# A hybrid layer on one core: x, four weights and B in one chain of loads, gates moved forward, Toeplitz matrices copied inside SBUF, C loaded once, and TensorE's order fixed in the output stage

## The chip, the core and the metric

The kernel runs on one core of a Trainium2 chip. The metric is the device time of one execution in microseconds (us); less is better. TensorE (PE) does the matmuls, VectorE (DVE), ScalarE (ACT) and GpSimd (POOL) the rest, and DMAs are issued from queues that belong to SyncE (SP), ACT or POOL.

## What is computed

One layer on x of 512 positions by 1024 columns, in float32. h = RMSNorm(x) goes through one projection w_in whose columns are split among a state-space branch with a gate, an attention branch with three head groups and a gate, and two merge gates:

```
h = rms_norm(x, norm_w)
u_s, z_s, q, k, v, z_a, r_s, r_a = split(h @ w_in)
y_s = s5_branch(u_s, lam, log_dt, b, c, d_skip, w_glu)      # GLU(GELU(Re(C h) + D u))
y_s = (y_s * silu(z_s)) @ w_ssm_out
y_a = dilated_attention(rope(norm(q)), rope(norm(k)), v)
y_a = (y_a * silu(z_a)) @ w_attn_out
m = sigmoid(r_s) * y_s + sigmoid(r_a) * y_a
out = x + m @ w_o
```

The state-space branch has 64 groups of 16 channels and 64 complex states each. Its recurrence runs over the 512 positions with a diagonal matrix that does not depend on the data.

## The kernel before, in words

Every product that matters is three fp32r matmuls: both sides are split into a high part and a low part, and mm3 (lines 107 to 110) adds high by high, high by low and low by high. cm_unit (line 180) makes 128 output columns for all 512 positions in 24 matmuls. `plan` fixes the order of the weights; load_w (line 170) loads one from SP into two rotating buffers `w_raw`, ACT makes `w_hi` (line 93), DVE makes `w_lo` (line 95). A Tile scheduler orders each engine's instructions from the program and its own estimates; POOL, ACT and SP each serve their list in order, and so do their DMA queues.

The stages follow one another:
- **Start** (196 to 240): x in four pieces, sums of squares, scaling (224), transposes to hT and their split. SP's list mixes the loads of x, the first two weights, the lambdas, B in four loads (419 to 422), positions and norm weights.
- **u units** 0 to 7 (264), and beside them the lambda chain on DVE, whose powers reach TensorE as atp and ftp and come back as AT and fT; from these and B come BB and BB2 on POOL and DVE.
- **W and X units** (271, 283): coefficients `ab` (coef, 252), their transposes (wps, 279), a copy W, and the input of the scan.
- **Scan** on DVE (589 to 648). TensorE runs gates ("fillers") meanwhile: `order` has za, zs, V of head pair 0, rs and two ra.
- **M stage** (675 to 793). For j = 0 to 7: ca_unit makes the output coefficients from C; m_unit makes kps on TensorE, copies it to `kt` on ACT (710), adds the diagonal on POOL (711), stores it to DRAM (kd, 712) and reads it back as the Toeplitz matrix (dd<-kd, 715); s_unit copies the scan's states (728, 729); y_unit makes yps from both (739, 741); g_unit transposes ysb and does the GELU in ACT and DVE. The gates' outputs go to DRAM (gd, rad) from SP (472, 478, 486).
- **GLU and w_ssm_out**, then **attention** over four head pairs: q and k of three groups, their turning (qtp, 847), scores with softmax (903 to 967), values (970: transposes ptp, then ot). Group weights are made on DVE (948 to 956) and moved across partitions by 16 POOL copies (960). V of pairs 1 to 3 is computed together with the third group of q and k.
- **The end**: w_attn_out with the gate loads `ral` (1108), and w_o with the residual xr (1117).

## Time and profile before

| | us |
|---|---|
| median of 3 runs | 746.56 (746.32 to 746.74) |
| profiled execution | 746.7 |
| its span | 744.9 |
| TensorE busy | 695.5 (93%) |
| DVE busy | 463.3 (62%) |
| ACT busy | 338.0 (45%) |
| POOL busy | 170.8 (23%) |

The span is the time from the first to the last record; 1.8 us lie around it. TensorE's busy share is a mean over stages, and a matmul counts as busy at either level of its clock: mean granted clock 0.975 of 2.4 GHz. So what is to be read is where TensorE waits, what for, and in which stretches the granted clock is 0.50. A wait row gives the instruction that waits, what ended the wait, the sum, how many times and the longest.

### The profile page before, as it was taken

Reading aid. Unit: us, or ns where it says so; the run is one execution under the profiler, and the core shown is the slowest. Engines: PE = TensorE matmul, PEld = TensorE weight load, DVE = VectorE, ACT = ScalarE, POOL = GpSimd, SP = SyncE. Lnnn points to the kernel's source line nnn. Section 1 sums busy time; section 2 is a strip of 40 time slices with the busy share of each in tenths; the row PEclk is TensorE's granted clock in tenths of the full one; section 3 lists DMA queues with packets and bytes.
Section 4 is the critical chain, followed back from the end, with each engine's and each line's share of the span. In section 5 each row is a group of like instructions: output and inputs, shape, how many; then the busy total and the mean of one; then the engine's idle time right before and its main releaser. Section 6 shows DMA issues by size and latency. Waiting matters only on the chain.

```text
span 744.9 us, 11696 instructions
## 1 busy us (share of the span) xinstructions
PE 695.5 (93%) x4357; PEld 573.2 (77%) x4357; DVE 463.3 (62%) x914; ACT 338.0 (45%) x662; POOL 170.8 (23%) x304
## 2 busy tenths in 40 slices
PE   2699999999989679999999999999989999999997
PEld 2687778788867467888888888878868877877886
DVE  6768756988957455575334658755764765463842
ACT  6443444334388475333144446537253733443310
POOL 3445642110011000551000315221511250230000
PEclk9899999999989889999999999999999998999999
DMA  9753644675636755455423332212312230326441
GB/s 204 128 147 105 162 110 101 120 177 147 117 103 125 137 123 149 132 165 167 141 60 114 103 96 72 85 45 71 95 48 69 71 90 28 114 71 240 157 142 56
DMA packets 153802, 85.41 MB, mean 115 GB/s; under 512 B 41097, under 2 KB 142865, under 8 KB 153617
## 3 DMA queue, kind: packets, MB, share of 16 engines
q1 hardware_dynamic: 153728, 84.66, 43.8%
q8 instruction: 34, 0.56, 0.3%
q14 instruction: 24, 0.19, 0.1%
q10 hardware_dynamic: 16, 0.00, 0.0%
HBM read 73.18 MB, written 11.47 MB: 114 GB/s over the span
## 4 chain that ended last, share of the span: by engine, by line
PE 81%; DMA 5%; ACT 4%; SPq 4%; DVE 3%; issue 1%; POOL 1%; ACTq 0%; DVEq 0%; POOLq 0%
PE pj L108 23%; PE pj L109 23%; PE pj L110 23%; PE ptp L1004 2%; PE ot L990 2%; DMA kd<-kt 1%; DMA dd<-kd 1%; DMA ral<-rad 1%; PE yps L739 1%; PE sps L934 1%; PE xps L290 1%; DMA gd<-th 1%; PE qtp L847 1%; PE yps L741 1%; PE wps L279 1%
## 5 line engine op out<-in xcount | busy, mean ns | idle before, releaser
L93 ACT ACTIVATE w_hi<-w_raw 128x1024 fp32r<-128x1024 f32 x100 | 106.0, 1061 | 239.2 <-PE pj L109 104.9
L95 DVE TENSOR_TENSOR w_lo<-w_raw,w_hi 128x1024 fp32r<-128x1024 f32 x98 | 124.8, 1274 | 106.5 <-ACT w_hi L93 105.8
L108 PE MATMUL pj<-hT_hi,w_hi 128*128 128x512 f32 (+1 forms) x344 | 134.2, 393 | 12.6 <-ACT w_hi L93 5.9
L109 PE MATMUL pj<-hT_lo,w_hi 128*128 128x512 f32 (+1 forms) x344 | 132.9, 387 | 0.7 <-DVE hT_lo L236 0.7
L110 PE MATMUL pj<-hT_hi,w_lo 128*128 128x512 f32 (+1 forms) x344 | 132.8, 387 | 0.0
L109 PE MATMUL pj<-w_lo,hT_hi 128*128 128x512 f32 (+1 forms) x288 | 106.1, 368 | 0.0
L108 PE MATMUL pj<-w_hi,hT_hi 128*128 128x512 f32 (+1 forms) x288 | 105.8, 369 | 0.0
L110 PE MATMUL pj<-w_hi,hT_lo 128*128 128x512 f32 (+1 forms) x288 | 105.1, 368 | 0.0
L108 PEld LDWEIGHTS pj<-hT_hi,w_hi 128*128 128x128 f32 x344 | 66.5, 195 | 27.5 <-ACT th L477 6.2
L109 PEld LDWEIGHTS pj<-hT_lo,w_hi 128*128 128x128 f32 x344 | 66.4, 193 | 13.7 <-DVE hT_lo L236 1.2
L110 PEld LDWEIGHTS pj<-hT_hi,w_lo 128*128 128x128 f32 x344 | 66.1, 192 | 13.7 <-DVE w_lo L95 0.3
L108 PEld LDWEIGHTS pj<-w_hi,hT_hi 128*128 128x128 f32 x288 | 54.1, 188 | 9.5 <-issue 0.2
L110 PEld LDWEIGHTS pj<-w_hi,hT_lo 128*128 128x128 f32 x288 | 54.1, 188 | 9.1
L109 PEld LDWEIGHTS pj<-w_lo,hT_hi 128*128 128x128 f32 x288 | 54.1, 188 | 8.6
L913 ACT ACTIVATE Pt<-Pt,st 128x256 f32<-128x256 f32 (+1 forms) x64 | 31.0, 491 | 18.5 <-DVE st L911 18.5
L834 POOL TENSOR_TENSOR rt<-qraw,tC 128x256 f32<-128x256 f32 x12 | 14.3, 1190 | 87.0 <-DVE qraw L828 86.7
L856 DVE SCALAR_TENSOR_TENSOR qkp<-qtp,wcol,qkp 128x512 fp32r<-128x512 f32 (+1 forms) x32 | 23.0, 746 | 13.4 <-ACT qkp L855 13.3
L943 POOL COPY sw<-st 32x4 f32<-32x4 f32 x64 | 12.0, 187 | 72.3 <-ACT Pt L913 69.5
L855 ACT ACTIVATE qkp<-qtp,wcol 128x512 fp32r<-128x512 f32 (+1 forms) x32 | 20.8, 686 | 15.6 <-PE qtp L847 10.2
L108 PE MATMUL pj<-gT_hi,w_hi 128*128 128x512 f32 x64 | 24.9, 391 | 1.4 <-ACT th L485 1.4
L262 DVE TENSOR_TENSOR ab<-ab 128x576 f32<-128x576 f32 (+1 forms) x24 | 22.0, 917 | 5.8 <-POOL ab L261 5.5
L109 PE MATMUL pj<-gT_lo,w_hi 128*128 128x512 f32 x64 | 24.9, 389 | 0.0
(275 smaller groups left out, 1336.2 us busy)
## 6 DMA issues: line engine op xcount, KB each, us to landing
w_raw<-in_w_in_dram SPq DMA_DIRECT2D x40, 512.0 KB
w_raw<-in_w_in_dram SPq DMA_DIRECT2D x112, 128.0 KB
dd<-kd SPq DMA_DIRECT2D x8, 512.0 KB
w_raw<-in_w_glu_dram SPq DMA_DIRECT2D x8, 512.0 KB
w_raw<-in_w_ssm_out_dram SPq DMA_DIRECT2D x8, 512.0 KB
w_raw<-in_w_o_dram SPq DMA_DIRECT2D x8, 512.0 KB
x_all<-in_x_dram SPq DMA_DIRECT2D x4, 512.0 KB
ud<-uT SPq DMA_DIRECT2D x8, 256.0 KB
```

Source lines behind the costliest of these rows:

```text
L93: act.activation(hi, src, AF.Copy, scale=scale)
L95: e.tensor_tensor(lo, src, hi.bitcast(F32), op=ALU.subtract)
L108: pe.matmul(o, lh, rh, start=first, stop=False, skip_group_check=True)
L109: pe.matmul(o, lh, rl, start=False, stop=False, skip_group_check=True)
L110: pe.matmul(o, ll, rh, start=False, stop=last, skip_group_check=True)
L262: dve.tensor_tensor(dst, dst, tv, op=ALU.add)
L834: pool.tensor_tensor(t1, rh[:, :, :, 0:16], cv.broadcast_to([P, NB * 2, 2, 16]), op=ALU.mult)
L855: act.activation(hi, ps[sl], AF.Copy, scale=w)
L856: dve.scalar_tensor_tensor(lo, ps[sl], w, hi.bitcast(F32), op0=ALU.mult, op1=ALU.subtract)
L913: act.activation(o, o, AF.Exp, bias=nm, scale=-1.0, accum_out=st[:, kind, 1, h, b:b + 1])
L990: pe.matmul(o, v, pts[h][:, (2 * i + k) * P:(2 * i + k + 1) * P], start=first, stop=kind == 1 and b == NB - 1 and k == 1, skip_group_check ...
L1004: pe.transpose(ps[:, (2 * i + k) * P:(2 * i + k + 1) * P], Pt[:, h, kind, 2 * bb + i, k * P:(k + 1) * P], ident)
```

## The change

The parts, in the program's order:
- x, four weights (one tile `w_early`) and B go out on SP in one chain; B is loaded in two DMAs, and its swapped copy D2 is made inside SBUF by two DMAs from POOL. The small loads move to POOL's queue. Two of four sums of squares move to DVE. ACT and DVE follow the written order through sums, scaling, weight splits and transposes; the lambda chain comes behind that, and atp/ftp behind the units u3 and u4.
- `order` starts with rs and seven ra, then za and zs. V leaves the list: V of head pairs 0 and 3 is made by itself in attention ("alone"), and only gate ra 7 is left for the end. One gate stands between W units.
- C is loaded once; p_unit makes the transposed C from one transpose and two matmuls, and both scaled copies on ACT; ca is made one unit further ahead, in four buffers.
- The Toeplitz matrix is filled by eight DMAs kt to dd inside SBUF, issued by POOL, into tiles set to zero once; kd is gone. kt lies at partitions 0 and 32 in turn, the diagonal comes from one load. The loads of u for y (uss) go out on POOL, the gates' stores of th on ACT.
- s_unit has four copies of 64x256 for eight, g_unit one DVE instruction less.
- The scan is spread over 13 gates for 10, two gates follow, and then each j has a gate, m_unit(j+2), y_unit(j), p_unit(j+4) and g_unit(j-1), each tied behind TensorE's last instruction by `queued`.

```diff
+    def queued():
+        return tc.issue_after(last[0].ins)
...
-    n_ra = 2
+    n_ra = 7
...
-    order = [("za", c) for c in range(NP)] + [("zs", c) for c in range(KT)] + [("v0", 0), ("v", 0)]
-    order += [("rs", c) for c in range(KT)] + [("ra", c) for c in range(n_ra)]
+    order = [("rs", c) for c in range(KT)] + [("ra", c) for c in range(n_ra)]
+    order += [("za", c) for c in range(NP)] + [("zs", c) for c in range(KT)]
...
+    alone = (0, NP - 1)
     for hp in range(NP):
         plan += wide_spec(w_in, head(Q0, 0, hp), head(K0, 0, hp), head(Q0, 1, hp), head(K0, 1, hp))
-        if hp == 0:
+        if hp in alone:
             plan += tok_spec(w_in, head(Q0, 2, hp), head(K0, 2, hp))
-            plan.append(cm_spec(w_in, RA0 + n_ra * P))
         else:
             plan += wide_spec(w_in, head(Q0, 2, hp), head(K0, 2, hp), head(V0, 1, hp), head(V0, 2, hp))
-            plan.append(cm_spec(w_in, V0 + hp * P))
-    for c in range(n_ra + 1, KT):
+        plan.append(cm_spec(w_in, V0 + hp * P))
+        if hp in alone:
+            plan += tok_spec(w_in, head(V0, 1, hp), head(V0, 2, hp))
...
+    moves = [(x_t[r], xv[r]) for r in range(NB)]
+    moves += [(early[i], plan[i][0][0].rearrange("(k p) c -> p k c", p=P)) for i in range(4)]
+    moves += [(D1[0:64], b_re[0].rearrange("g n q -> n g q")), (D1[64:128], b_im[0].rearrange("g n q -> n g q"))]
+    prev = None
+    for o, i in moves:
+        if prev is None:
+            prev = sp.dma_start(o, i)
+        else:
+            with tc.issue_after(prev.ins):
+                n = sp.dma_start(o, i)
+            prev = n
+    pool.dma_start(D2[64:128], D1[0:64])
+    pool.dma_start(D2[0:64], D1[64:128])
...
+    in_order[0] = True
+    for r in range(3):
+        sum_sq(r)
+    scale_x(0)
+    sum_sq(3)
+    prefetch(1)
+    turn_x(0)
+    prefetch(2)
+    scale_x(1)
+    normed = dve.last
+    prefetch(3)
+    turn_x(1)
+    in_order[0] = False
+    normed = normed, act.last
...
+    for j in (3, 4):
+        u_unit(j)
+    behind_u = last[0]
     pool.memset(AT[:, 0, :, 8:9], 1.0)
     pool.memset(AT[:, 1, :, 8:9], 0.0)
-    for i in range(2):
-        ps = bank("atp")
-        for k in range(8):
+    with tc.issue_after(behind_u.ins):
...
-    for js in ((4,), (5, 6), (7, 8)):
+        {"za": za_unit, "zs": zs_unit, "rs": rs_unit, "ra": ra_unit}[kind](c)
+    for js in ((1,), (2, 3), (4,), (5, 6), (7, 8)):
...
+    cna = big.tile([P, 8, P], F32, name="cn", tag="s6a")
+    sp.dma_start(cna[:, :, 0:64], c_re[0].rearrange("(j g) p n -> (g p) j n", j=8))
+    sp.dma_start(cna[:, :, 64:128], c_im[0].rearrange("(j g) p n -> (g p) j n", j=8))
...
-        pool.tensor_tensor(kt[:, :, T - 1, :], kt[:, :, T - 1, :], dg, op=ALU.add)
-        sp.dma_start(kd[j, :, :, 0:128], kt.rearrange("q g k p -> q g (k p)"))
-        M = (D1, D2, BB2)[j % 3].rearrange("p g q -> p (g q)")
-        kj = kd[j]
-        sp.dma_start(M.rearrange("p (g k) -> p g k", g=8),
-                     bass.AP(tensor=kj.tensor, offset=kj.offset, ap=[[Q, T], [8 * 240, Q], [240, 8], [1, P]]))
-        M = M.rearrange("p (g k) -> p g k", g=8)
+        pool.tensor_tensor(kt[:, :, T - 1, :], kt[:, :, T - 1, :], dg[rows], op=ALU.add)
+        M = Mb[j % 3]
+        for t in range(T):
+            pool.dma_start(M[Q * t:Q * t + Q, :, 0:P - Q * t], kt[:, :, t:].rearrange("q g k p -> q g (k p)"))
...
-                o = Sv[64 * a:64 * a + 64, h]
-                x_ = Xsv[64 * h:64 * h + 64, a, 4 * j:4 * j + 4]
-                act.copy(o[:, :, :, 1:NI], x_[:, :, :, 0:NI - 1])
-                act.copy(o[:, :, 1:NJ, 0], x_[:, :, 0:NJ - 1, NI - 1])
-        return Ss
+                act.copy(Sv[64 * a:64 * a + 64, h, :, 1:C + 1].rearrange("p g (j i) -> p g j i", j=NJ),
+                         Xsv[64 * h:64 * h + 64, a, 4 * j:4 * j + 4])
...
-        act.activation(q, s, AF.Square)
-        dve.tensor_scalar(q, q, 0.044715, 1.0, op0=ALU.mult, op1=ALU.add)
-        dve.tensor_tensor(q, q, s, op=ALU.mult)
+        act.activation(q, s, AF.Square, scale=math.sqrt(0.044715))
+        dve.scalar_tensor_tensor(q, q, 1.0, s, op0=ALU.add, op1=ALU.mult)
...
-    n_scan = 10
+            Ms[j] = m_unit(j, cas[j])
+    n_scan = 13
...
+    cas[3] = ca_unit(3)
+    for _ in range(2):
+        with queued():
+            filler()
     for j in range(8):
+        if fill:
+            with queued():
+                filler()
         if j + 2 < 8:
-            Ms[j + 2] = m_unit(j + 2, cas[j + 2], dgs[j + 2])
-        filler()
-        ysbs[j] = y_unit(j, cas.pop(j), Ms.pop(j), Us.pop(j), Ss_.pop(j))
-        if j + 3 < 8:
-            cas[j + 3], dgs[j + 3] = ca_unit(j + 3)
+            with queued():
+                Ms[j + 2] = m_unit(j + 2, cas[j + 2])
+        with queued():
+            ysbs[j] = y_unit(j, cas.pop(j), Ms.pop(j), Us.pop(j), Ss_.pop(j))
+        if j + 4 < 8:
+            with queued():
+                p_unit(j + 4)
+            cas[j + 4] = ca_unit(j + 4)
...
-            g_unit(j - 1, ysbs.pop(j - 1))
-    if fill:
-        filler()
+            with queued():
+                g_unit(j - 1, ysbs.pop(j - 1))
...
+    def v_alone(hp):
+        V = new_v()
+        finv = v0_unit(hp, V)
+        v_granule(hp, V)
+        finv()
+        return V
...
+        if hp == NP - 1:
+            V = v_alone(hp)
+            values(hp, Pt, V)
+            for c in range(n_ra, KT):
+                ra_unit(c)
+            continue
+        raws = qk_first()
+        if hp + 1 in alone:
+            raw = qk_third(turns)
+            values(hp, Pt, V)
+            qk_turn(2, raw, *QK)
+        else:
```

SP, the start. x_all is x, w_raw and w_early are weights, dd<-in_b the loads of B, scr the small inputs; the rows run from the last piece of x to the third weight. Before:

```order
L201 DMA x_all<-in_x_dram 128x1024
L306 DMA scr<-in_lam_re_dram 64x64
L307 DMA scr<-in_lam_im_dram 64x64
L308 DMA scr<-in_log_dt_dram 64x1
L419 DMA dd<-in_b_re_dram 64x64x16
L420 DMA dd<-in_b_im_dram 64x64x16
L421 DMA dd<-in_b_im_dram 64x64x16
L422 DMA dd<-in_b_re_dram 64x64x16
L490 DMA scr<-in_positions_dram 128x4
L524 DMA scr<-in_q_norm_w_dram 128x192
L526 DMA scr<-in_k_norm_w_dram 128x192
L174 DMA w_raw<-in_w_in_dram 128x8x128
```

Now:

```order
L259 DMA x_all<-in_x_dram 128x1024
L262 DMA x_all<-in_x_dram 128x1024 x3
L262 DMA w_early<-in_w_in_dram 128x8x128 x4
L262 DMA dd<-in_b_re_dram 64x64x16
L262 DMA dd<-in_b_im_dram 64x64x16
L217 DMA w_raw<-in_w_in_dram 128x8x128 x2
```

The third weight stood behind ten other loads, B among them; it is now inside a row of four weights ahead of B.

POOL, one unit of the M stage. dg is the diagonal, kt the row of the Toeplitz matrix, dd the tile that holds the matrices, uss the u and state inputs of yps, cn the C rows. Before:

```order
L697 TENSOR_TENSOR dg<-dg,ident 16x128
L682 COPY cn<-cn 128x64
L681 COPY cn<-cn 128x64
L711 TENSOR_TENSOR kt<-kt,dg 16x8x16
L722 MEMSET uss 128x8
```

Now:

```order
L785 TENSOR_TENSOR dg<-ident,dcol 16x128
L796 TENSOR_TENSOR kt<-kt,dg 16x8x16
L330 DMA uss<-ud 128x8x64
L807 MEMSET uss 128x8
L800 DMA dd<-kt 16x1024
L800 DMA dd<-kt 16x8x112
L800 DMA dd<-kt 16x8x96
L800 DMA dd<-kt 16x8x80
L800 DMA dd<-kt 16x8x64
L800 DMA dd<-kt 16x8x48
L800 DMA dd<-kt 16x8x32
L800 DMA dd<-kt 16x8x16
```

The C copies are gone from POOL's list, and a load of uss and eight copies kt to dd have come in, with the load ahead of the copies.

PE, the last head pair. sps are the scores, pj<-hT a gate, ptp the transposes of the probabilities, vtp those of V, ot the values. Before, at the last scores:

```order
L109 MATMUL pj<-hT_lo,w_hi 128x512
L934 MATMUL sps<-qkp 128x256 x12
L110 MATMUL pj<-hT_hi,w_lo 128x512
L108 MATMUL pj<-hT_hi,w_hi 128x512
L109 MATMUL pj<-hT_lo,w_hi 128x512
```

Now:

```order
L88 MATMUL pj<-aT,w_lo 128x512
L88 MATMUL sps<-qkp 128x2x128 x6
L88 MATMUL sps<-qkp 128x128 x3
L88 MATMUL sps<-qkp 128x256 x3
L88 MATMUL sps<-qkp 128x128 x3
L88 MATMUL sps<-qkp 128x256 x15
L92 MATMUL vtp<-ident,vt 128x128 x4
L92 MATMUL ptp<-ident,Pt 128x128 x10
L88 MATMUL ot<-ptb,V 64x4x32
```

Before, gates stood ahead of the last scores and behind them; now the last scores, V's transposes, the probabilities' transposes and the values stand next to one another.

## Rows read from the trace of the kernel before

**Rows 1.** TensorE's waits: instruction, what ended it; sum us, times, longest us.

```profile
PE pj L108 <- ACT w_hi L93: 5.9, 1, 5.9
PE pj L108 <- ACT th L477: 5.3, 2, 5.1
PE qtp L847 <- DVE qkp L856: 3.5, 2, 1.8
PE kps L706 <- DVE ab L262: 3.3, 1, 3.3
PE yps L741 <- ACT uss L729: 3.0, 1, 3.0
PE wps L279 <- DVE ab L262: 2.7, 2, 2.1
PE yps L739 <- DMA dd<-kd: 2.5, 1, 2.5
...
PE pj L108 <- DVE ral L1113: 1.1, 1, 1.1
PE ptp L1004 <- DVE qkp L856: 0.9, 2, 0.5
```

**Rows 2.** Windows at clock 0.50: length; busy PE, PEld, DVE, ACT, POOL; clock; DMA.

```profile
27.92:34.75 6.83, 3.61 (x15) 3.31 (x16) 6.18 (x36) 4.72 (x10) 3.25 (x8) 0.50 0.69 188
...
246.38:253.20 6.82, 5.36 (x13) 4.21 (x14) 5.17 (x8) 3.32 (x5) 1.03 (x4) 0.50 0.59 126
...
270.27:273.68 3.41, 3.41 (x60) 2.88 (x61) 0.69 (x1) 2.73 (x7) 0.04 (x1) 0.50 0.52 97
615.01:621.84 6.83, 6.37 (x32) 4.86 (x31) 3.25 (x5) 2.12 (x5) 0.00 (x0) 0.50 0.21 62
```

**Rows 3.** Chain of work, 0 to 36 us: start, us, what.

```profile
24.74 5.23 DMA w_raw<-in_w_in_dram
```

**Rows 4.** Chain of work, 236 to 275 us.

```profile
254.72 0.23 PE pj L108
254.96 0.34 PE kps L706 x8
255.30 0.27 PE yps L739 x4
...
258.29 2.44 DMA kd<-kt
260.74 9.26 DMA dd<-kd
```

**Rows 5.** Windows of 10 us over the M stage: one of them, and the sum.

```profile
215.00:225.00 10.00, 9.86 (x117) 7.49 (x114) 6.08 (x10) 9.65 (x23) 1.95 (x4) 0.97 0.34 81
...
sum 100.00, PE 84.20 PEld 67.34 DVE 54.04 ACT 66.97 POOL 12.47; mean PE 8.42 PEld 6.73 DVE 5.40 ACT 6.70 POOL 1.25
```

**Rows 6.** ACT's groups by form, 205 to 297 us: busy, mean ns; idle before.

```profile
L728 ACT COPY uss<-Xs 64x224 f32<-64x224 f32 x30 | 17.5, 585 | 4.8 <-PE yps L741 4.4
...
L729 ACT COPY uss<-Xs 64x28 f32<-64x28 f32 x32 | 7.6, 236 | 0.2
```

**Rows 7.** Instructions on the tile kt: ns least, median, most; first and last start.

```profile
L711 POOL TENSOR_TENSOR kt<-kt,dg x8: 440/450/962, 136.3 to 273.6; 16x128 f32<-16x128 f32 x8
L712 SPq DMA_DIRECT2D kd<-kt x8: 602/609/2447, 137.1 to 274.1; - x8
```

**Rows 8.** Timeline of DVE, 56 to 64 us: start, us, instruction.

```profile
59.96 2.94 DVE L432 TENSOR_TENSOR dd<-dd,ab 128x1024 f32<-128x1024 f32 x1 [1.83 <-POOL ab L430]
...
62.93 1.21 DVE L435 TENSOR_TENSOR dd<-dd,ab 128x1024 f32<-128x1024 f32 x1
```

**Rows 9.** Timeline of PE, DVE and POOL at the last head pair's softmax.

```profile
659.84 0.98 PE L934 MATMUL sps<-qkp 64*128 64x256 f32 x12
...
664.80 0.17 DVE L956 TENSOR_TENSOR sd<-sd,slt 128x16 f32<-128x16 f32 x1
...
665.04 5.19 POOL L960 COPY sfb<-sd 32x2 f32<-32x2 f32 x16 [7.71 <-DVE sd L956]
```

More of the change, by code (lines that the diff above doesn't have):

```diff
@@ L56, in tile_hybrid_block, with __init__, __getattr__, call @@
     nc = tc.nc
-    pe, act, dve, pool, sp = nc.tensor, nc.scalar, nc.vector, nc.gpsimd, nc.sync
+    pool, sp = nc.gpsimd, nc.sync
+    in_order = [False]
+    class Traced:
+        def __init__(self, eng):
+            self.eng = eng
+            self.last = None
+        def __getattr__(self, name):
+            f = getattr(self.eng, name)
+            if not callable(f):
+                return f
+            def call(*a, **k):
+                r = f(*a, **k)
+                if in_order[0] and name != "dma_start":
+                    if self.last is not None:
+                        tc.add_manual_dep(r.ins, self.last.ins.name, NOSYNC, reason="in order")
+                    self.last = r
+                return r
+            return call
+    NOSYNC = mybir.DependencyInfo(mybir.DependencyClass.NoSync, mybir.DependencyReason.DATA)
+    act, dve = Traced(nc.scalar), Traced(nc.vector)
+    last = [None]
+    class pe:
+        @staticmethod
+        def matmul(*a, **k):
+            last[0] = nc.tensor.matmul(*a, **k)
+        @staticmethod
+        def transpose(*a, **k):
+            last[0] = nc.tensor.transpose(*a, **k)
+    def queued():
+        return tc.issue_after(last[0].ins)
     dbg = dbg or {}
@@ L448, in wx @@
                 x_unit(j - 1, Ws.pop(j - 1))
-    for j in range(3, 8):
+    for j in range(5, 8):
         u_unit(j)
-        wx(*((), (), (0,), (1,), (2, 3))[j - 3])
+    wx(0)
     sza = cst.tile([P, NP, S], F32, name="sza")
@@ L530, in tile_hybrid_block @@
-    wps = bank("wcp")
-    for g in range(NG):
-        for a in range(2):
-            wd = sml.tile([1, 2, HD], F32, name="wd", bufs=2)
-            pool.tensor_copy(wd, qkw[0:1, a, g].unsqueeze(1).broadcast_to([1, 2, HD]))
-            pe.matmul(wps[:, 2 * g + a:2 * g + a + 1], wd.rearrange("p a d -> p (a d)"), ident[0:1, 0:1],
-                      start=True, stop=True, skip_group_check=True)
-    dve.tensor_copy(wcol.rearrange("p g a -> p (g a)"), wps[:, 0:6])
-    pool.memset(wcol[0:16], 1.0)
@@ L683, in ca_unit, with p_unit @@
+    Mb = [t.rearrange("p g q -> p (g q)").rearrange("p (g k) -> p g k", g=8) for t in (D1, D2, BB2)]
+    for t in (D1, D2, BB2):
+        pool.memset(t, 0.0)
+    cat = big.tile([P, nca // 2], F32, name="cat", tag="s7b")
+    p12s = {}
+    def p_unit(j):
         ps = bank("cps")
-        for i in range(2):
-            pe.transpose(ps[:, i * P:(i + 1) * P], cn[:, i], ident)
+        pe.transpose(ps[:, 0:P], cna[:, j], ident)
+        for h in range(2):
+            pe.matmul(ps[64 * h:64 * h + 64, P:2 * P], cna[:, j, 64 - 64 * h:128 - 64 * h], ident, start=True, stop=True,
+                      skip_group_check=True)
```

310 lines of the change are left out of this document (154 added, 156 removed).

## The prediction

> **What bounds the kernel now.** I read the view of TensorE's waits first, since the page shows TensorE busy through nearly every slice: all that a change can gain here is its idle time, and the time in which it works at the lower of its two clock levels. The waits [rows 1] lie at five places: the third weight of the start (5.9 us), the first W units (wps, 2.7), the first output of the state-space part (yps on uss, 3.0), the M stage (5.3 on th, 3.3 before kps, 2.5 on dd<-kd), and attention (3.5 and 0.9 over two head pairs, 1.1 on ral at the end). The wait ahead of the very first transposes is left out: the change does not shorten the chain before it.
>
> Then the windows with a granted clock of 0.50, which is 1.2 GHz [rows 2]. Of each I count half of TensorE's busy time as lost: 1.8 us after the start's wait, 2.7 + 1.7 + 1.7 in the M stage (a third stretch there is like the 3.41 us one), 3.2 in attention. Each stands behind a wait. In these traces a wait of 2.5 us or more was always followed by one, and of the two shorter attention waits one was.
>
> Last the chain of work. In the M stage it is not TensorE at all: the matrix goes kt to kd in DRAM (2.44 us) and kd to dd (9.26 us) [rows 4], and the store gd<-th, which holds ACT's next th, stands between them.
>
> **The change part by part.** The profiled execution took 746.7 us, 0.14 above the median, so its terms are used as they are.
>
> *Start.* Four weights now stand on SP right behind x. The third weight's DMA, which started only at 24.74 us [rows 3] behind B, the lambdas, positions and norm weights, goes out some 20 us earlier. Gone: 5.9 of wait and 1.8 of clock, 7.7 us. Given back: ACT and VectorE follow a written order in which the second half of x is scaled behind the first half's transposes and two weight splits, so hT of that half is late instead; weight 0 lands behind all of x; the lambda chain waits for hT and atp for the unit u4. No row shows that wait. It is 5.7 at most if the late half costs nearly all that was won, and 0 if VectorE keeps up. I take 3.4, near the middle. Gain 4.3, bounds 2 and 7.7.
>
> *W units.* A gate stands between W units, which covers the second W's wait; the first W keeps its own, and POOL has two memsets and two dg products ahead of its coefficients. Of the 2.7 I take half as gained: 1.4, bounds -2 and 2.7.
>
> *Scan.* Between the last X unit and the first y unit the order holds about 13 matmuls of 0.23 us [rows 4] less than before (a V granule moved into attention; gates and the queued units came in), so TensorE arrives 3.0 us earlier. VectorE gets the coefficients of unit 3 into this stretch and loses four z products and the three p copies. Its order is bound by the scan, as the 3.0 us wait shows. Against this, it no longer waits for the C loads and the p copies there. I take 0, bounds -5 and 3.
>
> *M stage.* The DRAM round trip goes, and one gate lies between two y units. Gone: 5.3 + 3.3 + 2.5 of wait and 6.1 of clock, 17.2 us. What is next? Per unit TensorE has 24 matmuls of 0.23, 32 yps of 0.068, 8 kps in 0.34 to 0.4 [rows 4], and the small transposes: 5.6 + 2.2 + 0.4 + 0.6 = 8.8 us. ACT was busy 67.0 us over eight such units, and 9.65 of 10 us in one window [rows 5]. The copies of s_unit fall from 4 x (0.585 + 0.236) = 3.3 us [rows 6] to four of 64x256, by a straight line through these two rows 0.64 each, 2.6; a second p copy comes in for four units. So ACT stays near 8.4 on average and above 9 in the units that carry p. I give back 2 (bounds 0 and 4), and 1 us for the last transposes, which now stand directly behind the last y unit with nothing between but one another (0 to 3).
>
> POOL is the new queue. Per unit it has a dg product, a kt add (0.45), a memset, one uss load and eight copies kt to dd. No row shows a DMA issued by POOL. The nearest row is SP's issue of the same kind of transfer, kd<-kt, 0.61 us, with 2.45 at worst [rows 7]. At 0.6 a unit costs POOL 9 x 0.6 + 1.2 = 6.6 us, under TensorE's 8.8. M(j) is asked for two units ahead. Only the last is tight: the load for y7 waits on POOL for y5's end, its eight copies stand behind that load, and from y5's end to y7 there are 5.6 + 2.2 + 0.5 = 8.3 us, against 6.6 + 2.4 for the landing: 0.7 us. At 2.45 the queue sets the stage (first rival). Sum of the stage: 17.2 - 2 - 1 - 0.7 = 13.5; bounds 4 and 17 without that rival.
>
> By the Trainium skill (SBUF — State Buffer, "SBUF: two separate sides") such a DMA can fare far worse: GpSimd writes its descriptors through the port pair that VectorE locks in some modes, and a transfer of about 620 ns took about 3100. As an estimate from that figure, an issue of 3.1 us would make 29 us a unit and the whole kernel about 855 us. The only sign of a shared port in this trace is milder: VectorE's 128x1024 product took 2.94 us beside a POOL product and 1.21 behind it [rows 8].
>
> *Attention.* V of head pairs 0 and 3 is now computed by itself, and seven gates have moved forward, so one gate is left for the end. Gained at pair 3's start: half of the 3.5 qtp wait and of the 0.9 ptp wait, 3.2 of clock: 5.4. Lost: 1.2 for narrower granules (about five matmul times of 0.23); then the softmax of pair 3. The order now ends it with 30 score matmuls in a row, four transposes of V, and then the probabilities' transposes. The last score matmuls of before end at 659.84 + 0.98 = 660.8; VectorE needs until 664.97 for the group weights, and POOL's sixteen copies run 5.19 us from 665.04 [rows 9]. Before, gates and the first rows of the output projection covered that. Exposed now: 4.6 to the first transposes (664.97 and the first scaling), then 3.0 of the POOL copies beyond the some 2.6 us of value matmuls of the first kind: 7.6 (bounds 3 and 10), and 1.7 of clock as behind every such wait. The ral loads still stand behind the residual's load, and 9 matmuls of 0.23 fewer lie ahead of them: 2.0 more than the 1.1 now. Sum: 5.4 - 1.2 - 7.6 - 1.7 - 2.0 = -7.1; bounds -10 and 2.
>
> **Sum:** 4.3 + 1.4 + 0 + 13.5 - 7.1 = 12.1 gained; 746.7 - 12.1 = 734.6, and 734.5 against the median. I say 734.5.
>
> **The rivals.**
> 1. *POOL's queue takes the place of the DRAM round trip* (slower). M7 is ready 1.5 us + six units of POOL + 2.4 after the loop's first kps; TensorE could start y7 after 57 us (four units of 9.3, two of 8.8, and the tail). For: 64 issues in a stretch where VectorE is busy 54% [rows 5], each of which may meet it. If 54% of them pay the 1.73 us by which 2.94 exceeds 1.21, an issue costs 1.54, a unit 15.1, M7 comes at 94.6, 37.6 late: 734.5 - 0.7 + 37.6 = 771. It decides from 1.1 us an issue on: there a unit is 11.1, M7 comes at 70.5, and the wait of 13.5 eats the whole gain. Against: nearest row 0.61; VectorE's work in this stage reads mostly one or two operands for 0.7 us, not 128x1024 pairs. What the Trainium skill states of descriptors (the page named above) is this rival's far end.
> 2. *The waits move rather than go*: the scan ends late (-5) and the end of attention costs its full bound (-2.9 more). For: VectorE is at its limit in the scan. 734.5 + 5 + 2.9 = 742.4.
> 3. *Everything is covered*: the start gives 7.7, ACT costs nothing in the M stage, pair 3's softmax only 3: 734.5 - 3.4 - 2 - 4.6 = 724.5. Against: ACT's 9.65 of 10.
> 4. *TensorE's order is fixed but the M stage still waits in each unit* for th or kps, because ACT is served in another order than TensorE asks: half of the 17.2 stays, 743. The order puts kt's four copies behind th, so a late th holds M too.
>
> **How the numbers follow.** My forecast, 734.5 (728 to 741): 0.42. Rival 1: 0.20. Rivals 2 and 4, near 743: 0.20 together, a quarter of it within 0.2% of now. Rival 3: 0.18. Two in ten may be left out: the upper half of rival 1 (above 755) and the far end of rival 3 (below 719) are. Range 719 to 755. A measurement here can tell about 0.2%, 1.5 us, from no change. Faster 0.76, the same 0.05, slower 0.19.
>
> **What would show it.** Start: no wait on w_hi near 25 us; a wait on hT_lo or x_all instead. M stage: y units 9 us apart, no idle time above 1 us; if yps waits for POOL's DMAs instead, rival 1 holds, and the spacing of the copies is its price. Scan: the wait of the first yps, 3 us. Pair 3: TensorE idle ahead of ptp for some 5 us and again ahead of the second half; if it isn't, that term was mine to blame. ral: about 3 us. I am wrong if the M stage does not gain 8 us or more, or if the end of attention doesn't lose any.

## The result, and the profile after

The changed kernel took 748.5 us (median; 744.7 to 750.4) beside 746.0 us (744.6 to 748.6) for the kernel before on the same chip: ratio 1.0026, 95% interval 1.0013 to 1.0038. It is not 12 us faster; it is a little slower. The profiled execution has a span of 746.8 us, and TensorE ends at 743.0 (before: 741.1). Medians and ratios leave out three executions far outside the others: 991 and 1741 us of a1_uss_sp, 759.6 of c3_start.

TensorE's waits over the whole run, as in [rows 1] (what waited, what ended it, us in all, times, longest). The waits on w_hi (5.9), on th (5.3), before kps (3.3) and on dd<-kd (2.5) are gone; others stand in their place:

```profile
PE yps L88 <- ACT uss L73: 5.3, 2, 3.4
PE ptp L92 <- DVE Pt L73: 4.0, 1, 4.0
PE yps L88 <- DMA dd<-kt: 3.7, 2, 2.0
...
PE pj L88 <- DVE ral L73: 3.0, 1, 3.0
PE wcp L88 <- POOL wd L624: 2.7, 2, 1.8
...
PE qtp L92 <- DVE qkp L73: 1.8, 1, 1.8
```

Four of the seven windows at the lower clock, as in [rows 2] (length; busy PE, PEld, DVE, ACT, POOL; clock; DMA share; GB/s), of the changed kernel. The first follows the wait on uss, the second stands at the end of the M stage, the third behind the qtp wait of pair 2, the last behind the ptp wait:

```profile
225.95:232.78 6.83, 4.52 (x58) 3.84 (x59) 0.00 (x0) 4.44 (x9) 6.12 (x11) 0.50 0.69 136
287.39:297.63 10.24, 8.36 (x109) 7.14 (x105) 4.59 (x6) 8.29 (x14) 1.49 (x4) 0.50 0.44 101
560.46:567.28 6.82, 6.33 (x30) 4.51 (x29) 3.13 (x5) 2.12 (x5) 0.00 (x0) 0.50 0.19 54
666.27:673.10 6.83, 4.83 (x20) 3.69 (x20) 5.38 (x22) 1.73 (x6) 3.61 (x16) 0.50 0.01 2
```

For a balance by stage I cut both traces at the same places of the program: start, W units, scan, first y unit to the last g unit (M stage), the rest. The same view for the changed kernel, then for the kernel before; length less PE's busy time is idle (sums are of unrounded numbers):

```profile
0.00:60.00 60.00, 44.14 (x313) 37.40 (x314) 43.33 (x157) 28.59 (x45) 22.74 (x54) 0.97 0.75 169
60.00:135.00 75.00, 71.36 (x550) 57.07 (x549) 44.55 (x45) 32.81 (x54) 32.04 (x25) 0.98 0.50 124
...
215.00:298.37 83.37, 73.44 (x834) 58.98 (x832) 48.09 (x65) 63.07 (x116) 40.49 (x71) 0.90 0.58 122
298.37:743.03 444.66, 433.78 (x2416) 363.88 (x2416) 254.03 (x535) 184.15 (x376) 100.28 (x197) 0.98 0.31 94
```

```profile
0.00:60.00 60.00, 40.96 (x304) 36.89 (x305) 40.16 (x154) 30.22 (x48) 26.97 (x59) 0.94 0.74 161
60.00:125.00 65.00, 61.29 (x503) 49.75 (x502) 46.66 (x51) 30.06 (x49) 26.71 (x18) 0.97 0.49 117
...
205.00:296.00 91.00, 75.48 (x803) 60.10 (x801) 51.40 (x74) 64.46 (x142) 8.18 (x19) 0.89 0.60 125
296.00:741.08 445.08, 437.75 (x2316) 361.50 (x2316) 252.04 (x536) 186.47 (x383) 98.86 (x196) 0.99 0.33 102
```

In the table "clock" is half of the busy time at 0.50. The traces have no clock ahead of 17.7 us (before) and 14.3 us (after); TensorE's time there is counted as at the lower level, since the first 16 hps transposes of the kernel before took 3.67 us and the next 16 took 1.91. That is 2.4 and 1.5 us of the start's clock. What is left of the busy time is work at full clock. The two lines from 205 (215) us on are one stretch, parted by hand: the wait of the first y unit on uss and the slow window behind it, and all else.

| us | before: idle + clock | after: idle + clock | gained | forecast |
|---|---|---|---|---|
| Start | 19.0 + 4.2 | 15.9 + 3.1 | 4.3 | 4.3 |
| W units | 3.7 + 1.7 | 3.6 + 1.7 | 0.1 | 1.4 |
| First y unit (scan) | 3.0 + 3.0 | 5.3 + 2.3 | -1.5 | 0 |
| M stage | 12.5 + 6.1 | 4.6 + 4.2 | 9.8 | 13.5 |
| Attention and end | 7.3 + 3.2 | 10.9 + 7.3 | -7.7 | -5.9 |
| TensorE's work | 677.2 | 684.2 | -7.0 | -1.2 |
| Sum | | | -2.0 | 12.1 |

(Attention's -7.1 holds the 1.2 of work, which has its own line here.) So 14 us are missing: 5.8 of work (2.7 of it belong to the start, as is shown below under TensorE's work), 3.7 in the M stage, 4.6 in three small terms. The experiments ask for each where it went.

Each column is one execution, and its clock is not a fixed cost. Nine of the traces have the attention and the end of the changed kernel: their idle time there is 10.8 to 11.6 us, their clock anything from 1.7 to 10.4 (here 7.3).

### The profile page after: what moved, and what is told of

It is laid out like the page before. It is cut to its first block, busy times and chain, and to the rows that moved or that the text cites. A ratio compares the mean times of both kernels' runs of the same rounds, so it can differ in the third digit from the quotient of the medians.

```text
span 746.8 us, 11927 instructions
## 1 busy us (share of the span) xinstructions
PE 702.7 (94%) x4481; PEld 579.9 (78%) x4481; DVE 465.3 (62%) x902; ACT 333.3 (45%) x630; POOL 210.3 (28%) x368
## 4 chain that ended last, share of the span: by engine, by line
PE 78%; DMA 6%; DVE 6%; ACT 4%; POOL 3%; issue 2%; SPq 0%; POOLq 0%; ACTq 0%
PE pj L88 66%; PE ptp L92 3%; DMA dd<-kt 2%; PE sps L88 2%; PE ot L88 2%; DVE scr L73 1%; DMA w_early<-in_w_in_dram 1%; PE qtp L92 1%; PE xps L88 1%; DMA ral<-rad 1%; PE wps L92 1%; PE yps L88 1%; POOL dd L800 1%; DMA uss<-ud 1%; DVE w_lo L73 1%
## 5 line engine op out<-in xcount | busy, mean ns | idle before, releaser
L73 ACT ACTIVATE w_hi<-w_raw 128x1024 fp32r<-128x1024 f32 x96 | 101.9, 1062 | 228.4 <-PE pj L88 210.7
L88 PE MATMUL pj<-w_hi,hT_hi 128*128 128x512 f32 (+1 forms) x320 | 111.5, 349 | 0.0
L88 PE MATMUL pj<-w_lo,hT_hi 128*128 128x512 f32 (+1 forms) x320 | 111.2, 348 | 0.0
L88 PE MATMUL pj<-w_hi,hT_lo 128*128 128x512 f32 (+1 forms) x320 | 110.8, 348 | 0.0
L88 PEld LDWEIGHTS pj<-w_hi,hT_lo 128*128 128x128 f32 x320 | 60.1, 188 | 8.3 <-issue 0.2
L88 PEld LDWEIGHTS pj<-w_hi,hT_hi 128*128 128x128 f32 x320 | 60.0, 188 | 8.0
L88 PEld LDWEIGHTS pj<-w_lo,hT_hi 128*128 128x128 f32 x320 | 60.2, 188 | 7.2
L927 POOL TENSOR_TENSOR rt<-qraw,tC 128x256 f32<-128x256 f32 x12 | 15.9, 1322 | 102.0 <-DVE qraw L73 92.9
L800 POOL DMA_DIRECT2D dd<-kt x64 | 33.5, 531 | 10.3 <-DMA uss<-ud 8.8
L796 POOL TENSOR_TENSOR kt<-kt,dg 16x128 f32<-16x128 f32 x8 | 5.8, 725 | 88.1 <-ACT kt L73 88.0
L92 PE MATMUL ptp<-ident,Pt 128*128 128x128 f32 x120 | 21.8, 321 | 5.2 <-DVE Pt L73 4.0
```

The lines of the kernel that those rows point to most:

```text
L73: r = f(*a, **k)
L88: last[0] = nc.tensor.matmul(*a, **k)
L92: last[0] = nc.tensor.transpose(*a, **k)
L796: pool.tensor_tensor(kt[:, :, T - 1, :], kt[:, :, T - 1, :], dg[rows], op=ALU.add)
L800: pool.dma_start(M[Q * t:Q * t + Q, :, 0:P - Q * t], kt[:, :, t:].rearrange("q g k p -> q g (k p)"))
L927: pool.tensor_tensor(t1, rh[:, :, :, 0:16], cv.broadcast_to([P, NB * 2, 2, 16]), op=ALU.mult)
```

## The experiments

Fifteen kernels; each ratio is to the kernel before on the same chip, so they are compared by ratio. The changed kernel stands at 1.0026.

| run | edit on the changed kernel | median us | ratio (95%) |
|---|---|---|---|
| a1_uss_sp | uss loads on SP | 747.0 | 1.0008 (0.9980 to 1.0037) |
| a2_gate | last gate ahead of the last values | 745.3 | 0.9993 (0.9963 to 1.0022) |
| a3_c_turn | C turned by two transposes | 746.9 | 1.0010 (0.9983 to 1.0038) |
| a4_wx | W units 1 to 3 ahead of the gates | 744.3 | 0.9973 (0.9948 to 0.9997) |
| b1_four | these four | 738.1 | 0.9912 (0.9885 to 0.9940) |
| c2_five | four, and x loaded behind ral | 731.3 | 0.9802 (0.9770 to 0.9835) |
| b2_six | c2_five, kt copies on DVE | 730.5 | 0.9817 (0.9792 to 0.9843) |
| c4_six_free | b2_six, order not fixed in the M stage | 732.5 | 0.9817 (0.9785 to 0.9849) |
| c1_kt_half | c2_five, kt copies shared by ACT and DVE | 726.5 | 0.9754 (0.9719 to 0.9788) |
| d1_no_sp | c1_kt_half with the uss loads on POOL | 730.1 | 0.9806 (0.9770 to 0.9842) |
| d2_kt_sp | uss loads on SP, kt copies shared | 741.1 | 0.9933 (0.9909 to 0.9957) |
| d3_kt | kt copies shared, nothing else | 747.0 | 1.0018 (0.9993 to 1.0042) |
| b3_free | order not fixed in the M stage | 742.8 | 0.9975 (0.9955 to 0.9995) |
| b4_dram | DRAM round trip back | 762.8 | 1.0243 (1.0221 to 1.0265) |
| c3_start | start as before | 752.2 | 1.0075 (1.0049 to 1.0100) |

**Are the copies inside SBUF worth what I gave them?** One edit takes them back (the tile kd in DRAM and its zeros come back too):

```
-        for t in range(T):
-            pool.dma_start(M[Q * t:Q * t + Q, :, 0:P - Q * t], kt[:, :, t:]...)
+        sp.dma_start(kd[j, :, :, 0:128], kt...)
+        sp.dma_start(M, bass.AP(tensor=kj.tensor, offset=kj.offset, ap=[[Q, T], [8 * 240, Q], [240, 8], [1, P]]))
```

> The changed kernel with the Toeplitz matrices built by the round trip through DRAM again (two DMAs on SP for each unit, as in the kernel before) in place of the eight copies on POOL; order, C, gates and start as changed. Theory (the copies inside SBUF are worth what the M stage gained, some 9 to 10 us of the 18.7 us it waited): y matmuls wait on dd in four units or more by 8 to 14 us together, span 752 to 760. Rival (the matrices being built two units ahead in a fixed order hides the trip of 2.4 and 9.3 us as well as it hides the copies, and POOL's stall is gone): no wait on dd above 4 us together, span within 3 us of 746.8 or under it.

TensorE's waits of that run:

```profile
PE yps L88 <- DMA dd<-kd: 14.3, 3, 7.0
PE yps L88 <- ACT uss L73: 8.5, 2, 5.3
```

The trip costs 2.2 per cent, 16 us, in the new order. Building the matrices two units ahead does not hide it: the first y unit and the M stage lose 31.5 us of idle time and clock instead of 16.4 (kernel before: 24.6). So the M term had the right cause; what it lacked was what comes next.

**What comes next: two queues.** POOL's queue in the changed kernel, late in the M stage (start us, us, instruction, in brackets idle time before it and what ended it):

```profile
264.13 1.36 POOL L330 DMA_DIRECT2D uss<-ud  x1 [1.27 <-issue]
...
265.58 3.65 POOL L800 DMA_DIRECT2D dd<-kt  x7
270.52 0.53 POOL L800 DMA_DIRECT2D dd<-kt  x1 [1.28 <-DMA uss<-ud]
...
274.58 3.65 POOL L800 DMA_DIRECT2D dd<-kt  x7
281.84 0.53 POOL L800 DMA_DIRECT2D dd<-kt  x1 [3.60 <-DMA uss<-ud]
```

Seven copies go out at 0.53 us each, and the eighth waits until the uss load issued ahead of them has landed. The simplest cure is to give that load to SP:

```
-        eng = pool
         if Uj is None:
-            Uj, eng = t2k("Uj"), sp
-        eng.dma_start(Uj, ...)
+            Uj = t2k("Uj")
+        sp.dma_start(Uj, ...)
```

> The changed kernel with the loads of uss issued by SP instead of POOL; the eight copies kt to dd stay on POOL. Theory: in each M unit the eighth copy waits on POOL until the uss load issued by the same queue has landed (3.2, 1.3, 3.6 and 0.8 us of POOL idle in front of the last copy), and so the last two matrices come late. With the load gone from POOL these idle times go, the two waits of yps on dd<-kt (3.7 us) and the half clock around them (4.2 us) go: about 741 us. Rival one: the copies' own issue, 0.53 us each, and their landing set the end; then the waits stay and the time is within 1.5 us of the changed kernel's 748.5. Rival two: SP's list holds uss behind weight loads, and yps waits for uss instead: 748.5 or more.

TensorE's wait and POOL's copies in that run:

```profile
PE yps L88 <- DMA dd<-kt: 5.6, 1, 5.6
```

```profile
273.12 4.19 POOL L799 DMA_DIRECT2D dd<-kt  x8 [0.24 <-POOL uss L806]
282.73 0.46 POOL L795 TENSOR_TENSOR kt<-kt,dg 16x128 f32<-16x128 f32 x1 [5.42 <-ACT kt L73]
```

The stall is gone: eight copies go in one piece. The wait is not, and the time moved by 0.2 per cent, within its interval: now POOL stands 5.4 us for kt, from ACT. In the changed kernel the last kps had ended by 276.02, and ACT came to it at 281.35, in the order of its queue:

```profile
275.39 0.63 PE L88 MATMUL kps<-ab,dd 128*16 128x128 f32 x16
```

```profile
276.52 0.63 ACT L73 ACTIVATE gT_hi<-gq 128x512 fp32r<-128x512 f32 x1 [0.76 <-DVE gq L73]
277.06 1.31 ACT L73 COPY uss<-Xs 64x256 f32<-64x256 f32 x2
278.39 1.06 ACT L73 ACTIVATE w_hi<-w_raw 128x1024 fp32r<-128x1024 f32 x1
...
281.35 1.50 ACT L73 COPY kt<-kps 16x256 f32<-16x256 f32 x4
```

By unit, the kt copies begin 2.5, 0.8, 0.7, 2.4, 3.9 and 5.3 us behind the end of their kps: ACT falls back further in each of the last three, as the step "I give back 2" foresaw, but the price comes at the end, through kt. The cure is to share the copies:

```
-            act.copy(kv[:, a], ps[32 * a:...
+            (act.copy if a < 2 else dve.tensor_copy)(kv[:, a], ps[32 * a:...
```

> The changed kernel with the kt copies shared by the scalar engine and DVE alone, uss loads still on POOL. By the theory of two causes: POOL still stands 3 us before the eighth copy, the copies of the last unit end at most 2 us earlier, and the waits on dd stay at 2.5 us or more. By the rival (the late kt copies alone): the wait falls under 2 us as with both edits, and the two runs are equal.

> The changed kernel with two edits: uss loads on SP and the kt copies shared by the scalar engine and DVE. Theory (POOL's stall and the late kt copies are the two causes of the waits on dd, either alone leaves the other: with the loads on SP alone the wait was 5.6 us): the waits on dd at 284 to 290 us, 3.7 us, fall under 2, the half clock behind them (8.4 us busy at half) goes to under 3, and the median is 0.4 to 0.9 per cent under the changed kernel's. Rival (some later step of the M unit takes over, or yT on the scalar engine): waits on dd and yT together stay above 3 us, median within 0.3 per cent.

The wait on dd, of d3_kt and then of d2_kt_sp:

```profile
PE yps L88 <- DMA dd<-kt: 6.5, 1, 6.5
```

```profile
PE yps L88 <- DMA dd<-kt: 2.5, 1, 2.5
```

Either cure alone leaves the wait at 5.6 or 6.5 us; both bring it to 2.5, no window at the lower clock follows, and the median falls by 0.9 per cent, 7 us. In the traces the first y unit and the M stage lose 16.4 us in the changed kernel, 16.1 and 16.8 with one cure, 11.9 with both: 4.5 us, of which 3.6 are clock. The other 2.5 us of the median are not shown to come from there. The wait missed "under 2" by half a microsecond. The same shows from the other side, in the fastest version without the first cure:

> The fastest version so far (four edits, later load of x, kt copies shared by two engines) with the uss loads back on POOL, where they and the eight copies wait for each other. Theory (the POOL stall is a cause of its own, hidden in the changed kernel behind the scalar engine's lateness): POOL stands 3 us before the eighth copy of the later units again, the last y waits on dd by 3 us or more instead of 1.6, and the span is 2 to 6 us over 722.9. Rival (only the lateness of the kt copies counts; POOL's stall lies in time that TensorE does not miss): wait under 2 us and span within 2 us.

Its waits on dd are 7.1 us in two, against 1.6, and it is 0.5 per cent slower, though the intervals overlap. The two links are not quite apart: kt's copies begin up to 4.5 us behind their kps there, against 1.3.

**TensorE's work.** Records of cps (engine, operation, tiles, count, ns least/median/most, first to last start) in the changed kernel; the kernel before has 16 records, all transposes:

```profile
L88 PE MATMUL cps<-ident,cn x32: 272/323/476, 133.8 to 260.2; 128*64 128x128 f32 x32
...
L92 PE MATMUL cps<-ident,cn x8: 328/328/476, 133.5 to 259.8; 128*128 128x128 f32 x8
```

The swapped half of C is made by two 64-column matmuls against the identity, and each shows as two records. Counted to the next record's start, cps takes 5.3 us instead of 1.9. A layout re|im|re lets one transpose make it:

```
-    cna = big.tile([P, 8, P], ...)
+    cna = big.tile([P, 8, 192], ...)
+    sp.dma_start(cna[:, :, 128:192], c_re[0]...)
-        for h in range(2):
-            pe.matmul(ps[64 * h:64 * h + 64, P:2 * P], cna[:, j, 64 - 64 * h:128 - 64 * h], ident, ...)
+        for i in range(2):
+            pe.transpose(ps[:, i * P:(i + 1) * P], cna[:, j, 64 * i:64 * i + P], ident)
```

> The changed kernel with the swapped C made by a transpose, as before, instead of two fp32 matmuls against the identity (C's real part is loaded twice, into 192 columns a unit). Theory: TensorE's cps time falls from 5.8 to about 2 us. The four units ahead of the first y unit are hidden behind the scan, the four in the M stage are not: 1 to 2 us gained, about 747 us. Rival one: all of it is on the path: 744.7. Rival two: none is, because ACT sets the M stage's period: 748.5.

cps is back at 16 records and 1.8 us, the work at 681.3 instead of 684.2. The time moved by 0.2 per cent, within its interval, so only the trace shows this one.

By the same count another 3.4 us are in pj. pj has 2664 records instead of 2568, since 128x256 granules replace 128x512 ones, but these cost little: all matmuls of pj<-w,hT come to 179.2 us instead of 178.5. The rest, 2.7 us, lies in the 144 matmuls of 128x256 that both kernels have in their first u units: 20.2 us instead of 17.5. It is a wait of the start that the count takes for work. In the changed kernel the first of them come in groups of six, one group every 1.42 us, since ACT (hT_hi) and VectorE (hT_lo) make two pieces of hT in that time and wait on each other in turn:

```profile
17.64 0.38 PE L88 MATMUL pj<-hT_lo,w_hi 128*128 128x256 f32 x1
17.86 0.28 PE L88 MATMUL pj<-hT_hi,w_lo 128*128 128x256 f32 x1
...
18.54 0.38 PE L88 MATMUL pj<-hT_hi,w_hi 128*128 128x256 f32 x1
19.06 0.38 PE L88 MATMUL pj<-hT_lo,w_hi 128*128 128x256 f32 x1
```

```profile
17.10 0.88 DVE L73 SCALAR_TENSOR_TENSOR hT_lo<-hps,nwc,hT_hi 128x256 fp32r<-128x256 f32 x2 [0.54 <-ACT hT_hi L73]
18.01 0.84 ACT L73 ACTIVATE hT_hi<-hps,nwc 128x256 fp32r<-128x256 f32 x2 [0.58 <-DVE hT_lo L73]
```

In the kernel before VectorE made a piece every 0.46 us:

```profile
18.14 0.47 DVE L236 SCALAR_TENSOR_TENSOR hT_lo<-hps,nwc,hT_hi 128x256 fp32r<-128x256 f32 x1
18.60 0.47 DVE L236 SCALAR_TENSOR_TENSOR hT_lo<-hps,nwc,hT_hi 128x256 fp32r<-128x256 f32 x1
```

So the first 24 matmuls of the changed kernel take 6.3 us, from 14.62 to 20.90; from 22.74 on they come every 0.11 us. No run takes back the order of ACT and VectorE, so its worth in time is not shown.

**The scan.** Five gates now stand between the W units where three stood, so the last X unit ends at 133.6 us instead of 118.7, and the scan on DVE starts later. The edit brings W units 1 to 3 ahead of those gates, and two of the gates into the scan:

```
+    wx(1)
+    wx(2, 3)
-    for js in ((1,), (2, 3), (4,), (5, 6), (7, 8)):
+    for js in ((4,), (5, 6), (7, 8)):
...
-    n_scan = 13
+    n_scan = 15
```

> The changed kernel with the first two gates taken from between the W units and put into the scan (15 gates there instead of 13), as the kernel before had it. Theory: the time from the last X unit to the first y unit is set by the scan on VectorE, some 87 us and three more for the copies; the last X comes some 10 us earlier, the gates then cover the scan, and the wait of the first yps (5.3 us with 2.3 of half clock) goes, while up to 4 us of waits come back between the W units: 742 to 746 us. Rival: the wait of the first yps is set by ACT's copies and kt in its list, not by the scan's length: it stays, and the time is 748.5 or up to 4 us more.

The scan's first product over Xs, on DVE, in the changed kernel and in this run:

```profile
134.74 1.23 DVE L73 TENSOR_TENSOR scn<-Xs,scn 128x1024 f32<-128x1024 f32 x1 [2.00 <-ACT Xs L73]
```

```profile
125.14 1.23 DVE L73 TENSOR_TENSOR scn<-Xs,scn 128x1024 f32<-128x1024 f32 x1 [2.00 <-ACT Xs L73]
```

The 5.3 us wait of the first y unit is gone, the wcp wait too, and 2.4 us of xps on Uj and 2.0 of yps on its load are new. By stage it gains 7.4 us in the first y unit and the M stage and loses 2.7 at the W units. This edit alone gives 0.5 per cent.

**The end of attention.** One gate granule is put between the last scores and the last values:

```
+            scored = last[0]
             V = v_alone(hp)
+            with tc.issue_after(scored.ins):
+                for c in range(n_ra, KT):
+                    ra_unit(c)
             values(hp, Pt, V)
-            for c in range(n_ra, KT):
-                ra_unit(c)
```

> The changed kernel with the last gate (ra 7) held behind the last score matmul of head pair 3, so that it covers the softmax. Theory: the 4.0 us wait ahead of the first ptp goes to under 1 us, and the half clock behind it (2.4 us) with it: about 742 us. The ral wait (3.0 us) may stay, since the residual's load still stands ahead of the gate loads. Rival: the softmax chain only moves the wait behind the gate, or ral grows by as much; then it stays within 1.5 us of 748.5.

The ptp wait of 4.0 us falls away. New are 2.0 us of sps on qkp, 1.5 on aT and two of 0.3, and ral is 2.5 instead of 3.0, so idle time behind the M stage falls only from 10.9 to 10.3 us: the rival was right, the wait moved. The clock there falls from 7.3 to 3.2, but that lies within what nine traces without this edit show (1.7 to 10.4). The time moved by 0.3 per cent, and the intervals overlap, so a gain of this edit is not shown.

**Do they add up?**

> The changed kernel with the four edits tried singly together: the uss loads on SP, the last gate granule put between the last scores and the values, C turned by two transposes from an re|im|re layout, and three W units ahead of the gates that delay them. Theory (TensorE's own list sets the time: its work and the waits in it add up): the C edit takes 3.5 us of work, the W edit the wcp wait (2.7) and the two uss waits (5.3) with some 3 us of half clock behind them, less 2.4 us of a new wait of the X matmuls, the gate granule the ptp wait (4.0) with 2 to 3 us of clock; the loads on SP nothing by themselves. Sum 14 to 16 us: profiled span 731 to 734 where the changed kernel had 746.8, median 2 per cent under it, 1.5 to 2 per cent under the kernel before. Rival (the gains are taken back at the next wait, since the scalar engine or POOL paces the M stage): the y matmuls wait on the copies into dd by 8 us or more instead of 3.7, and the span stays above 740.

738.1 us, 1.1 per cent under the changed kernel: about the sum of the four ratios (0.2 + 0.3 + 0.2 + 0.5), and less than the traces had promised. The wait on dd is 5.5 us there, as in a1. Yet the rival was wrong on the place: the first y unit and the M stage lose 9.6 us instead of 16.4, and TensorE's work falls by 4.6. What the sum had too high is the end: idle time and clock behind the M stage are 18.4 us, as in the changed kernel (18.2), and 2.9 us are lost at the W units. Next come x and kt:

```
-            sp.dma_start(th, rad[c])
+            ral = sp.dma_start(th, rad[c])
...
+    with tc.issue_after(ral.ins):
         sp.dma_start(xr, ...)
```

> The four edits and the later load of x alone, kt copies all on the scalar engine. It parts the two edits by which the run with six was 7.6 us under the run with four. Theory (the later load of x took the 2.4 us ral wait and the half clock behind it, 3.4 us; the kt copies on DVE under 1 us of idle time, 5.5 to 4.7): median 732 to 735. Rival (the kt copies on DVE brought the most): 736 to 738, with no ral wait.

> The same four edits, and two more: the copies of kps into kt go from the scalar engine to DVE, and the load of the residual x is queued on SP behind the loads of ral. Theory (after the POOL stall is gone it is the scalar engine's queue that makes the last kt late: with the uss loads on SP the last four kt copies began 5.8 us after their matmuls had ended): the copies start within 2 us of their matmuls in every unit, no y matmul waits on dd by over 1 us, the ral wait (3.0) falls under 1: span 4 to 8 us under the one with four edits. Rival (the trip of the eight copies itself is what y7 waits for, or DVE is as late as the scalar engine): the last y still waits on dd by 2 us or more and the span is within 3 us of the other.

The load of x, 2 MB, stood ahead of the ral loads on SP. Behind them it costs nothing, no ral wait of TensorE is left, and the time falls by 1.1 per cent. Moving all kt copies to DVE brings nothing more (0.9817 against 0.9802): the wait on dd is still 4.7 us, and the last kt begins 5.1 us behind its kps. DVE is as late as ACT, so on the kt copies the rival of that run held. The third way shares them:

> The four edits and the later load of x, with the four kt copies of a unit shared: two on the scalar engine, two on DVE. Theory (neither in-order queue keeps up with TensorE's 9.0 to 9.4 us for a unit when it has all four: the scalar engine was busy 8.4 to 8.8 of 9.4 us with all, DVE 8.0 to 9.2, each with waits on the other between the steps of the gelu): shared, neither falls behind, the last unit's kt add starts within 5 us of its kps, and the last y waits on dd by 2.5 us or less (4.7 with all four on DVE): span 2 to 5 us under 730.3. Rival (the two halves wait for each other, or a copy's place behind the gelu's steps and not its length makes it late): the wait on dd stays at 4 us or more and the span is within 2 us of 730.

TensorE's wait on dd in this run, and one window of it, of 525 us at the higher clock throughout:

```profile
PE yps L88 <- DMA dd<-kt: 1.6, 1, 1.6
```

```profile
20.00:545.30 525.30, 508.38 (x3372) 418.86 (x3372) 361.85 (x641) 249.09 (x448) 173.45 (x259) 1.00 0.46 118
```

It is the fastest version, 2.5 per cent under the kernel before; its interval overlaps that of c2_five, not that of b2_six. Its balance is 33.0 idle, 4.2 clock, 682.0 work; the changed kernel's was 40.3, 18.5 and 684.2. Of 24 us between the two traces, 14 are clock. Some of that is chance: this trace has the highest mean clock of its six executions (0.998, the others 0.986 to 0.993), the changed kernel's the lowest of its twenty (0.973, the others to 0.984).

**The fixed order.** Every `with queued():` of the M stage is replaced by one that does nothing:

> The changed kernel with the fixed order of TensorE taken out of the M stage (the six places where a block is queued behind TensorE's last instruction), so that the scheduler orders it as in the kernel before; all else unchanged. Theory (the units being built two ahead is what removed the waits, the fixed order only keeps them there): kps and y matmuls are split and wait again, idle time between 205 and 300 us grows by 2 to 6 us and the span by as much, 748 to 753. Rival (the fixed order holds TensorE behind the first late unit, so it costs): idle time there falls by 3 us or more and the span is 743 or less. A third way, that it makes no difference: both within 2 us.

> The six edits (kt copies on DVE) without the fixed order of TensorE in the M stage. Theory (the fixed order costs TensorE some 3 us, as the run of the changed kernel without it was 743 instead of 748): 726 to 728.5. Rival (with the other five causes gone there is nothing late that a free order could fill): within 1.5 us of 730.5.

The free order made the changed kernel 0.5 per cent faster: TensorE puts a gate's matmuls into the first y unit instead of waiting 5.3 us in it, and the waits on dd grow from 3.7 to 8.5 us. In the version with six edits, in which no y unit waits for uss, it makes no difference. So what the fixed order cost in the changed kernel hung on that late unit: it made TensorE stand behind it.

**The start.** The order of the loads is put back: x, x, w, x, w, x, then B in four loads, then two weights. The small loads stay on POOL's queue, and ACT and VectorE keep the new order:

> The changed kernel with the loads of the start in the order of the kernel before (x, x, w, x, w, x, then B in four loads, then two weights). Theory (the start is worth its waits: 6 to 7 us of idle and half clock before 35 us): the third weight comes after 30 us, TensorE waits there 4 to 6 us, and the span is 4 to 7 us above 746.8, since no later wait of TensorE but the one at 222 us takes it up. Rival (the scan on DVE, which TensorE waits for at 222 us, is set by something else and takes it up): that wait shrinks by 3 us or more, and the span is within 2 us.

The median is 0.5 per cent over the changed kernel's, some 3.6 us, and the two intervals do not meet. The wait I named for the third weight did not come: with B alone ahead of it, it is early enough, and idle and clock of the first 60 us rise by 2.7 us through hT_lo (1.6) and scr (1.1) instead. Its profiled execution took 745.1 us, 7 under its median, so the trace says little on the whole; the worth of the loads' order, 3 to 4 us, is shown by the times, its way only in part.

## Why the prediction was wrong, step by step

- *Start, 4.3.* By the table right in size, 23.3 us of idle and clock became 19.0, but partly by luck. The 5.9 us on w_hi went as said. 1.1 us come from the first transposes, which start at 11.59 us instead of 12.68, and I had left them out. Of what was given back, the list of waits shows only 0.2 on hT_lo, which I had named; 2.7 us hide in TensorE's work, where the matmuls wait piece by piece for hT, and of the first half of x, not of the second. So the start gained 1.6.
- *W units, 1.4.* It is 0.1. The wps wait shrank as said, from 2.7 to 1.0 us, and the xps wait went. But TensorE's wcp products, fed by six POOL copies (wd), come at 76.1 to 92.7 us instead of 94.0 to 104.5 and now wait 2.7. I had counted POOL's memsets and dg products there and not these.
- *Scan, 0.* It is -1.5. "TensorE arrives 3.0 us earlier" looked at TensorE's side alone. The gates that were added ahead of the last X unit delay VectorE's start of the scan as well, which a4_wx shows. The slow windows at 208.83 to 215.66 us, behind this wait, and at 75.71 to 79.12 us in the kernel before were missing from my list.
- *M stage, 13.5.* It is 9.8. The copies are worth that and more (b4_dram). Idle time fell by 7.9 us, where 7.4 were forecast; the miss is the clock: I counted 6.1 as gone and 1.9 went. The step that failed is "only the last is tight ... 0.7 us". An issue costs 0.53 us, under the 0.6 I took from [rows 7], so rival 1 is out. But the eighth copy waits for a landing, and kt comes late from ACT's queue: 3.7 of wait at the last two units instead of 0.7, and 4.2 of clock, for which the sum had no term. Neither cause shows by its removal alone; both cures together bring 4.5 in the trace of d2_kt_sp.
- *Attention, -5.9 without the work.* It is -7.7, near by two errors that cancel. Idle time rose by 3.6 where 7.4 were forecast: the exposed softmax was sized at 7.6 from [rows 9] (its second part comes to 2.2 by those rows, not 3.0) and cost 4.0, since the second half of the values did not wait again for POOL's copies; ral came out at the 3.0 foreseen. The clock rose by 4.1 where I had it fall by 1.5. I counted the 3.2 us behind pair 3's wait as gained, but here a window stands behind the 1.8 us qtp wait of pair 2 (560.46 to 567.28), and two more behind ptp and ral. That varies between executions: the same qtp wait of 1.76 us stands in all 16 traces of the changed kernel and its variants, and a window follows it in seven.
- *TensorE's work, -1.2.* It is -4.3 without the start's 2.7. For C loaded once there was no term on TensorE at all, though the diff has two matmuls in place of one transpose: 3.4 us. That is the second step that failed, a term put at nothing. The narrower granules cost 0.7, less than the 1.2 forecast.

Both of my own signs of error stayed silent: the M stage gained over 8 us and the end of attention lost. The forecast fell through terms that no list of waits shows: the matmuls added for C, the slow pace of the first matmuls, and the lower clock behind waits that were new.

## What to carry to other kernels

When TensorE is busy 94 per cent of the time, count its matmuls before and after by form first; C's 3.4 us outweigh most waits here. Where matmuls come further apart than in a run of the same form, a busy engine is waiting. A transfer moved to another queue is priced by its issue, by what it waits for there, and by the engine that feeds it: the chain kps, kt, add, copies had two late links, and curing one showed nothing. A wait costs itself and often the lower clock behind it, and that part varies between executions of the same waits, so forecast it as a range.
